# A two-layer decoder trunk in float32: part of the input is turned by VectorE instead of TensorE, and the model dimension is renumbered to suit

## The chip, the cores and the metric

The kernel runs on one core of a Trainium2 chip. The engines that matter here are TensorE (PE; its weight loads have rows of their own, PEld), VectorE (DVE), ScalarE (ACT), GpSimd (POOL) and SyncE (SP), which issues nearly all DMAs. The metric is the device time of one execution in microseconds; a comparison uses the median of several runs.

## The reference, cut to what matters

```python
def reference(x, ...):                       # x (1, 1024, 1024) float32
    h = x
    # layer 0: HGRN2 mixer (w_in: 1024 -> 4096), layer norm, gated ConvFFN, layer norm
    mix = hgrn2_mixer(h, hgrn_w_in[0], lower_bounds[0], hgrn_gnorm_w[0], hgrn_w_out[0])   # h @ w_in first
    h = layer_norm(ALPHA * h + mix, ...)
    h = layer_norm(ALPHA * h + conv_ffn(h, ...), ...)
    k, v = split(h @ shared_w_kv)            # 1024 -> 512, once
    # layer 1: sliding-window attention (w_q: 1024 -> 1024), layer norm, gated ConvFFN, layer norm
    mix = swa_sink_mixer(h, k, v, swa_w_q[0], swa_sinks[0], bias, mask, swa_w_out[0])
    ...
    return h
```

Each product `h @ w` sums over the 1024 model features d. In which order and grouping the sum visits d is free, as long as h and w agree.

## The kernel before, in words

TensorE sums over partitions, so both operands of `h @ w` must have features on the 128 partitions. The weights lie so in memory (a row is a feature). The activations come as rows of tokens and must be turned: `T` holds the turned activations, `T[p, 0, kc, t]` the rounded high part and `T[p, 1, kc, t]` the low part of token t and feature 128·kc + p, for eight groups kc = 0..7 (`KC` = 8). A float32 product is made of three passes, high·high, high·low and low·high, so everything is split in two before it is multiplied. `split` does that: ScalarE writes the rounded copy (line 221), VectorE writes the difference (`low_part`, line 169).

The tokens are eight row blocks (`tb` = 0..7) of 128. `x_load` brings one block of x, 512 KB, into `Y[:, tb, :]`, tokens on partitions. `x_block` (blocks 0 and 1) and `turn_block` (blocks 2 to 7) turn a block: eight TensorE transposes (`tr`, line 204; the block's 128 by 128 piece is the stationary operand, the identity the moving one) into PSUM, then one split from PSUM into `T`. `turn_block` is also called by `ln_mid`, which turns the eight row blocks of h between the two layers; there the products with `shared_w_kv` and `swa_w_q` follow. The FFNs and the rest turn their data by code of their own.

The beginning of the program, in order. SyncE issues x block 0, two weight units `raw0` and `raw1` (512 KB each in two DMAs, `ig_load`), x blocks 1 to 5, the forget-gate weights `f`, x blocks 6 and 7, the query weights `q` and the masks. `first_rows` (line 752) multiplies blocks 0 and 1 while the weights are still being split; between its passes the generator `ahead` (`x_first`) places the transposes of blocks 1, 2 and 3. `ig_block` then does two row blocks per step, tp = 1, 2, 3 (lines 714 and 715: for each kc a 512-wide matmul with the high part of `T` and a 256-wide one with the low part), and during steps tp = 1 and 2 `x_pair` places the transposes of the next two blocks. After them `qf` multiplies with the f and q weights.

Every engine here works through its instructions in the order in which the program writes them (`tc.manual_schedule`). `od` (class `Order`) is a clock kept while the program is written: matmuls advance it, `od.spawn` starts a generator at a delay, and `od.tick` after each matmul group resumes those that are due. So the numbers behind `yield` and in `spawn` only set where instructions are written. `lower_bounds` computes a small table (`lbt`) from a transpose of `pr` (line 824) and some VectorE and ScalarE operations of 8 to 17 columns.

Of the kernel before, what the change touches and what calls it, by code (L numbers as in the profile page):

```python
# [13 lines left out]
AF = mybir.ActivationFunctionType  # L14
ALU = mybir.AluOpType

P = 128
S = 1024
D = 1024
NB = S // P  # L20
KC = D // P
# [86 lines left out]
def trunk(ctx: ExitStack, tc: tile.TileContext, a: dict, out: bass.AP):  # L108
    nc = tc.nc
    PS = bass.MemoryType.PSUM  # L110
    od = Order()
# [10 lines left out]
    nhalf = cp.tile([P, 1], F32, name="nhalf")  # L122
# [5 lines left out]
    T = cp.tile([P, 2, KC, S], F32R, name="T")  # L128
    Y = cp.tile([P, 8, D], F32, name="Y")
# [10 lines left out]
    def psmm():  # L140
        return mmp.tile([P, 512], F32, name="psmm")

    def psax():
        return axp.tile([P, 1024], F32, name="psax")
# [12 lines left out]
    def hl_at(i):  # L157
        return HL[:, 2 * i:2 * i + 2, :]
# [8 lines left out]
    def low_part(lo, src, hi, eng):  # L167

        make = lambda e: e.tensor_tensor(lo, src, hi.bitcast(F32), op=ALU.subtract)  # L169
        if isinstance(eng, list):  # L170
            eng.append(lambda: make(nc.vector))
        else:
            return make(eng or nc.vector)
# [29 lines left out]
    def tr(ps, src):  # L203
        nc.tensor.transpose(ps, src, ident)  # L204
        od.t += 0.109
# [14 lines left out]
    def split(hi, lo, src, eng=None):  # L220
        nc.scalar.copy(hi, src)  # L221
        return low_part(lo, src, hi, eng)
# [35 lines left out]
    def turn_block(tb):  # L258

        ps = psax()  # L260
        for kc in range(KC):
            tr(ps[:, kc * P:(kc + 1) * P], Y[:, tb, kc * P:(kc + 1) * P])
        ts = slice(tb * P, (tb + 1) * P)
        split(T[:, 0, :, ts], T[:, 1, :, ts], ps.rearrange("p (k t) -> p k t", k=KC))

    def ln_mid(tb):
        yield 11.0 if tb < 4 else 22.0
        turn_block(tb)
# [379 lines left out]

    x = a["x"][0]
    w_in = a["hgrn_w_in"][0]  # L650
    w_iv = w_in.rearrange("(kc p) c -> p kc c", p=P)
    hgrn_pool = tc.tile_pool(name="hp", bufs=1, reuse_waits="tile")
    with tc.tile_pool(name="t", bufs=1, reuse_waits="tile") as raws, hgrn_pool as hp:
        raw_tail(raws)

        def ig_load(h, u):
            return load(lambda r: [(r.rearrange("p (k g c) -> p k g c", k=4, g=2)[:, :, g, :],
                                    w_iv[:, 4 * u:4 * u + 4, (2 + g) * D + h * P:(2 + g) * D + (h + 1) * P])
                                   for g in range(2)])
# [4 lines left out]
        def qf_load(h, g):  # L664
            c0 = g * D + h * P
            return load(lambda r: [(r.rearrange("p (k c) -> p k c", k=KC), w_iv[:, :, c0:c0 + P])])
# [55 lines left out]
        def soon_all(left=0):  # L722
            while len(soon) > left:
                od.finish([soon.pop(0)])

        def ig_first(raw):

            hl = hl_at(ring["hl"] % 6)
            ring["hl"] += 1
            by_gate = lambda t: t.rearrange("p (k g c) -> p k g c", k=4, g=2)  # L730
            for g in range(2):
                nc.vector.tensor_copy(by_gate(hl[:, 0])[:, :, g, :], by_gate(raw)[:, :, g, :])
            low_part(hl[:, 1], raw, hl[:, 0], nc.gpsimd)
            return hl.rearrange("p h (k c) -> p h k c", k=4)

        def ig_second(raw):

            hl = hl_at(ring["hl"] % 6)
            ring["hl"] += 1
            for k in range(2):  # L740
                nc.scalar.copy(hl[:, 0, 512 * k:512 * (k + 1)], raw[:, 512 * k:512 * (k + 1)])
            low_part(hl[:, 1], raw, hl[:, 0], None)
            return hl.rearrange("p h (k c) -> p h k c", k=4)
# [26 lines left out]
        with tc.tile_pool(name="ep", bufs=1, reuse_waits="tile") as ep:  # L770
            pr = ep.tile([17, P], F32, name="pr")

            def x_load(tb):
                nc.sync.dma_start(Y[:, tb, :], x[tb * P:(tb + 1) * P, :])

            def x_block(tb):
                ts = slice(tb * P, (tb + 1) * P)
                halves = [psmm() for _ in range(2)]
                for k in range(KC):
                    tr(halves[k // 4][:, k % 4 * P:(k % 4 + 1) * P], Y[:, tb, k * P:(k + 1) * P])  # L780
                for i, ps in enumerate(halves):
                    ks = slice(4 * i, 4 * i + 4)
                    split(T[:, 0, ks, ts], T[:, 1, ks, ts], ps.rearrange("p (k t) -> p k t", k=4))

            def x_pair(tb):
                yield 0.0
                turn_block(tb)
                yield 0.5
                turn_block(tb + 1)

            warm = sm.tile([P, 1], F32, name="warm")
            mf = hp.tile([P, 7 * BL + P], F32, name="kd")
            nc.gpsimd.dma_start(pr[:16, :], a["hgrn_lb_logits"].rearrange("r (k p) -> (r k) p", p=P))
            nc.gpsimd.dma_start(pr[16:17, :], a["hgrn_gnorm_w"])
            with tc.manual_schedule(engines={EN.PE, EN.SP, EN.Activation, EN.DVE}):
                nc.scalar.activation(warm, nhalf, AF.Exp)
                x_load(0)
                raw0 = ig_load(0, 0)
                raw1 = ig_load(0, 1)
                for tb in range(1, 4):  # L800
                    x_load(tb)
                us = [ig_first(raw0)]
                lm = ep.tile([P, NH], F32, name="lm")
                le = ep.tile([P, 2, NH], F32, name="le")

                idle = psmm()
                for n in (9, 3):
                    for _ in range(n):
                        nc.tensor.matmul(idle[:, :P], still, still, start=True, stop=True)
                    if n == 9:  # L810
                        x_block(0)
                us.append(ig_second(raw1))

                def x_first():
                    x_block(1)
                    yield 1.0
                    turn_block(2)
                    yield 1.2
                    turn_block(3)

                def lower_bounds():
                    yield 0.0
                    ps = psmm()
                    nc.tensor.transpose(ps[:, :17], pr, ident[:17, :17])
                    nc.vector.tensor_copy(par, ps[:, :17])
                    nc.vector.tensor_tensor(lm, par[:, 0:8], par[:, 8:16], op=ALU.max)
                    for r in range(2):
                        nc.vector.tensor_tensor(le[:, r, :], par[:, 8 * r:8 * r + 8], lm, op=ALU.subtract)
                    nc.scalar.activation(le, le, AF.Exp)
                    nc.scalar.activation(warm, nhalf, AF.Sigmoid)  # L830
                    nc.vector.tensor_tensor(lm, le[:, 0, :], le[:, 1, :], op=ALU.add)
                    nc.vector.reciprocal(lm, lm)
                    nc.vector.tensor_tensor(lbt[:, 0, :], le[:, 0, :], lm, op=ALU.mult)
                    nc.vector.tensor_scalar(lbt[:, 1, :], lbt[:, 0, :], -1.0, 1.0, op0=ALU.mult, op1=ALU.add)

                bounds = od.spawn(lower_bounds(), 4.9)
                ahead = x_first()
                ig_block(0, us, 0, ahead=ahead)
                od.finish([od.spawn(ahead), bounds])
                for tb in range(4, 6):  # L840
                    x_load(tb)
                raws0 = {"f": qf_load(0, 1)}
                for tb in range(6, NB):
                    x_load(tb)
                raws0["q"] = qf_load(0, 0)
                nc.sync.dma_start(mf, a["masks"])
                w0 = {}
                for tp in range(1, NB // 2 - 1):
                    ahead = od.spawn(x_pair(2 * tp + 2), 2.0)
                    ig_block(0, us, tp)  # L850
                    od.finish([ahead])
                    soon_all(1)
                w0["f"] = qf_split(raws0["f"])
                ig_block(0, us, NB // 2 - 1)
                w0["q"] = qf_split(raws0["q"])
                soon_all()
                nc.vector.tensor_copy(msk, mf)
# [347 lines left out]
        with tc.manual_schedule(engines={EN.PE, EN.SP, EN.Activation, EN.DVE, EN.Pool}):  # L1205
# [89 lines left out]
            ps = psax()  # L1295
# [26 lines left out]
    with (tc.tile_pool(name="ta", bufs=1, reuse_waits="tile") as raws,  # L1322
# [6 lines left out]
        sk, nsk = sinks[:, :16], sinks[:, 16:32]  # L1329
        nc.scalar.dma_start(sk, bass.AP(tensor=a["swa_sinks"].tensor, offset=0, ap=[[0, P], [1, 16]]))  # L1330
        wkv = a["shared_w_kv"]
        wkvv = wkv.rearrange("(kc p) c -> p kc c", p=P)
        Kl = at.tile([P, 2, S], F32R, name="Kl")
        Vt = at.tile([P, NB, 256], F32, name="Vt")
        khl, uv = [], []
# [25 lines left out]
            proj_tok(uv, tp, ps)  # L1361
            nc.scalar.copy(Vt[:, 2 * tp:2 * tp + 2, :], ps.rearrange("p (a b) -> p a b", a=2))

        wq = a["swa_w_q"][0].rearrange("(kc p) (h e) -> p kc h e", p=P, e=64)

        W0 = at.tile([P, 2, 4, P], F32, name="W0")
        bfs = {}
# [145 lines left out]
        with tc.manual_schedule(engines={EN.PE, EN.Activation, EN.DVE, EN.Pool}):  # L1513
# [7 lines left out]
            q, done = next(g)  # L1521
# [20 lines left out]
            for c in range(8):  # L1542
                fill = q_proj(hl) if c < 7 else last_filler()
                nq, nd = next(fill)
                for bp in range(0, 4, 2):
                    n = 2 * c + bp // 2
# [48 lines left out]
                q = nq  # L1595
            for _ in range(2):
                ps = psax()
# [49 lines left out]
```

## Time and profile before

| | |
|---|---|
| median of 3 runs | 2131.9 us (2131.87 to 2132.25) |
| the profiled execution | 2131.04 us, span 2129.3 us |
| PE busy | 2119.9 us (100%), 12663 matmuls |
| PEld busy | 1779.6 us (84%) |
| DVE busy | 1760.9 us (83%) |
| ACT busy | 926.5 us (44%) |
| POOL busy | 132.5 us (6%) |
| PE clock granted | 0.999 |
| DMA | 278.96 MB, mean 131 GB/s |

A row of the page's groups names line, engine, operation, output<-inputs, shape and count, then busy time and mean duration of one, then the idle time before it and what ended that. In names of matmuls the moving operand stands first behind the arrow, the stationary one second. A row of the chain that ended last has start, length and what ran; lengths there do not overlap, so they add up to the span. In the windows view each engine's busy time in a stretch is given with its number of instructions.

### The profile page before, as it was taken

Reading aid. Unit: us, or ns where it says so; the run is one execution under the profiler, and the core shown is the slowest. Engines: PE = TensorE matmul, PEld = TensorE weight load, DVE = VectorE, ACT = ScalarE, POOL = GpSimd, SP = SyncE. Lnnn points to the kernel's source line nnn. Section 1 sums busy time; section 2 is a strip of 40 time slices with the busy share of each in tenths; the row PEclk is TensorE's granted clock in tenths of the full one; section 3 lists DMA queues with packets and bytes.
Section 4 is the critical chain, followed back from the end, with each engine's and each line's share of the span. In section 5 each row is a group of like instructions: output and inputs, shape, how many; then the busy total and the mean of one; then the engine's idle time right before and its main releaser. Section 6 shows DMA issues by size and latency. Waiting matters only on the chain.

```text
span 2129.3 us, 32129 instructions
## 1 busy us (share of the span) xinstructions
PE 2119.9 (100%) x12663; PEld 1779.6 (84%) x12663; DVE 1760.9 (83%) x2375; ACT 926.5 (44%) x1491; POOL 132.5 (6%) x150
## 2 busy tenths in 40 slices
PE   9999999999999999999999999999999999999998
PEld 8888888888888888888888888888888888888887
DVE  4777776677999999887988658969999999978986
ACT  4444444452444444434433356743544444444430
POOL 1000000001100000000001113321000000000002
PEclk9999999999999999999999999999999999999999
DMA  5655443214223222228854411042233222249662
GB/s 216 243 211 169 144 132 119 75 32 177 99 85 98 85 89 79 80 99 275 288 190 161 129 26 45 24 149 89 80 100 98 90 86 83 86 148 325 229 215 90
DMA packets 229838, 278.96 MB, mean 131 GB/s; under 512 B 29960, under 2 KB 158648, under 8 KB 226872
## 3 DMA queue, kind: packets, MB, share of 16 engines
q1 hardware_dynamic: 228736, 276.53, 39.0%
q8 instruction: 99, 1.62, 0.3%
q10 hardware_dynamic: 856, 0.37, 0.1%
q14 instruction: 51, 0.42, 0.1%
q0 software_dynamic: 96, 0.02, 0.0%
HBM read 213.94 MB, written 62.94 MB: 130 GB/s over the span
## 4 chain that ended last, share of the span: by engine, by line
PE 99%; DMA 0%; DVE 0%; SPq 0%; issue 0%; DVEq 0%
PE psmm L194 17%; PE psmm L196 17%; PE psmm L195 17%; PE psax L194 10%; PE psax L196 10%; PE psax L195 10%; PE psmm L714 5%; PE psax L200 4%; PE psmm L715 3%; PE psmm L204 1%; PE psmm L200 1%; PE psax L204 1%; PE psax L1427 1%; PE psmm L1274 1%; DMA Y<-in_x_dram 0%; PE psmm L752 0%
## 5 line engine op out<-in xcount | busy, mean ns | idle before, releaser
L194 PE MATMUL psmm<-T,HL 128*128 128x512 f32 x768 | 303.4, 395 | 0.0
L196 PE MATMUL psmm<-T,HL 128*128 128x512 f32 x768 | 299.4, 390 | 0.0
L195 PE MATMUL psmm<-T,HL 128*128 128x512 f32 x768 | 299.2, 390 | 0.0
L473 DVE SCALAR_TENSOR_TENSOR Y<-Y,cwt 128x1023 f32<-128x1023 f32 (+1 forms) x176 | 225.0, 1281 | 44.3 <-ACT Y L471 42.9
L221 ACT CAST HL<-rx 128x1024 fp32r<-128x1024 f32 (+1 forms) x151 | 150.7, 1007 | 178.3 <-PE psmm L195 30.9
L169 DVE TENSOR_TENSOR HL<-rx,HL 128x1024 fp32r<-128x1024 f32 (+1 forms) x151 | 178.5, 1188 | 16.9 <-ACT HL L221 16.8
L714 PE MATMUL psmm<-HL,T 128*128 128x512 f32 x496 | 176.8, 399 | 0.0
L196 PEld LDWEIGHTS psmm<-T,HL 128*128 128x128 f32 x768 | 144.2, 188 | 30.7
L194 PEld LDWEIGHTS psmm<-T,HL 128*128 128x128 f32 x768 | 144.3, 188 | 29.6 <-issue 0.4
L195 PEld LDWEIGHTS psmm<-T,HL 128*128 128x128 f32 x768 | 144.3, 188 | 28.8 <-issue 0.4
L471 ACT ACTIVATE Y<-Y,cwt 128x1024 f32<-128x1024 f32 x88 | 108.7, 1238 | 101.6 <-DVE Y L460 89.4
L715 PE MATMUL psmm<-HL,T 128*128 128x256 f32 x496 | 138.9, 280 | 0.0
L194 PE MATMUL psax<-T,HL 128*128 128x512 f32 x352 | 137.3, 390 | 0.0
L196 PE MATMUL psax<-T,HL 128*128 128x512 f32 x352 | 137.0, 389 | 0.0
L195 PE MATMUL psax<-T,HL 128*128 128x512 f32 x352 | 137.0, 389 | 0.0
L243 POOL TENSOR_TENSOR rs<-rs,nhalf 128x1 f32<-128x1 f32 x32 | 44.6, 1394 | 1286.6 <-DVE rs L242 1286.6
L714 PEld LDWEIGHTS psmm<-HL,T 128*128 128x128 f32 x496 | 93.1, 188 | 21.0
L715 PEld LDWEIGHTS psmm<-HL,T 128*128 128x128 f32 x496 | 93.7, 189 | 0.4
L221 ACT CAST HT<-rx 128x1024 fp32r<-128x1024 f32 (+1 forms) x37 | 35.5, 960 | 127.9 <-DVE rx L427 76.4
L169 DVE TENSOR_TENSOR HL<-raw,HL 128x1024 fp32r<-128x1024 f32 x51 | 62.1, 1219 | 20.2 <-ACT HL L176 19.3
L195 PEld LDWEIGHTS psax<-T,HL 128*128 128x128 f32 x352 | 66.2, 188 | 13.7
L196 PEld LDWEIGHTS psax<-T,HL 128*128 128x128 f32 x352 | 66.1, 188 | 13.6
(315 smaller groups left out, 5232.3 us busy)
## 6 DMA issues: line engine op xcount, KB each, us to landing
rx<-in_ffn_w_in_dram SPq DMA_DIRECT2D x136, 256.0 KB, 3.2
rx<-gd SPq DMA_DIRECT2D x118, 256.0 KB, 3.9
Y<-in_ffn_w_out_dram SPq DMA_DIRECT2D x44, 512.0 KB, 6.4
bsd<-Y SPq DMA_DIRECT2D x22, 1024.0 KB, 4.8
gd<-Y SPq DMA_DIRECT2D x44, 512.0 KB, 2.6
rx<-in_ffn_w_out_dram SPq DMA_DIRECT2D x54, 256.0 KB, 4.7
R<-bsd SPq DMA_DIRECT2D x44, 256.0 KB, 5.1
Y<-in_ffn_w_in_dram SPq DMA_DIRECT2D x40, 256.0 KB, 2.9
```

The lines of the kernel that those rows point to most:

```text
L169: make = lambda e: e.tensor_tensor(lo, src, hi.bitcast(F32), op=ALU.subtract)
L194: nc.tensor.matmul(ps, st(0), mv(0), start=start, stop=False)
L195: nc.tensor.matmul(ps, st(0), mv(1), start=False, stop=False)
L196: nc.tensor.matmul(ps, st(1), mv(0), start=False, stop=stop)
L200: nc.tensor.matmul(ps, lhsT, rhs, start=start, stop=stop, **kw)
L204: nc.tensor.transpose(ps, src, ident)
L221: nc.scalar.copy(hi, src)
L243: nc.gpsimd.tensor_tensor(rs, rs, nhalf, op=ALU.pow)
L471: nc.scalar.activation(c, u, AF.Identity, bias=cwt[:, l, 3, ci:ci + 1], scale=cwt[:, l, 2, ci:ci + 1])
L473: nc.vector.scalar_tensor_tensor(c[:, sh:], u[:, :S - sh], cwt[:, l, 2 - sh, ci:ci + 1], c[:, sh:], op0=ALU.mult, op1=ALU.add)
L714: nc.tensor.matmul(ps, T[:, 0, kc, ts], w[:, :, kc % 4, :], start=kc == 0, stop=False)
L715: nc.tensor.matmul(ps[:, :256], T[:, 1, kc, ts], w[:, 0, kc % 4, :], start=False, stop=kc == KC - 1)
```

## The change

Four things change together.

1. Features are grouped as 8p + k instead of 128·k + p: `T[p, ., k, t]` now holds feature 8p + k. `turn_block` and `x_block` therefore take `Y[:, tb, kc::KC]`, every eighth column, as stationary operand, and the weights `hgrn_w_in`, `shared_w_kv` and `swa_w_q` are read by `"(p kc) c -> p kc c"`, eight neighbouring rows per partition.
2. x blocks 3 to 7 are no longer turned by TensorE. Their loads put column quarter q (256 columns) onto partitions 32q to 32q + 31, with token t of a 32-token group on partition 32q + t (`quarters`: four DMAs, one block at a time for block 3, two blocks at a time for 4, 5 and 6, 7). A VectorE transpose of 32 by 32 squares (`turn_squares`, line 274 after) then gives the turned block in one instruction, written over `Y[:, tb - 3, :]`, which is free by then. It reads every eighth column within a square, 32 bytes apart, and writes contiguously.
3. The split of these blocks (`split_turned`) reads the turned block from SBUF instead of PSUM.
4. The order at the beginning is rewritten: SyncE issues all of blocks 3 to 5 before f; the transpose of `pr` moves ahead; `lower_bounds` is cut in two around its ScalarE operation; the turn of block t + 1 stands behind the split of block t.

```diff
 def turn_block(tb):
-            tr(ps[:, kc * P:(kc + 1) * P], Y[:, tb, kc * P:(kc + 1) * P])
+            tr(ps[:, kc * P:(kc + 1) * P], Y[:, tb, kc::KC])
...
+    def quarters(to, rows):
+        for q in range(4):
+            nc.sync.dma_start(to[q * 32:(q + 1) * 32].rearrange("p (b d) -> p b d", b=rows.shape[0] // 32),
+                              rows[:, q * 256:(q + 1) * 256].rearrange("(b t) d -> t b d", t=32))
+    def turn_squares(src, turned):
+        nc.vector.transpose(turned.rearrange("p (k b t) -> p b k t", k=KC, b=4),
+                            src.rearrange("p (b d k) -> p b k d", b=4, k=KC))
+        od.vec(1.1)
+    def split_turned(tb, turned):
+        ts = slice(tb * P, (tb + 1) * P)
+        split(T[:, 0, :, ts], T[:, 1, :, ts], turned.rearrange("p (k t) -> p k t", k=KC))
+        od.vec(1.2)
...
-    w_iv = w_in.rearrange("(kc p) c -> p kc c", p=P)
+    w_iv = w_in.rearrange("(p kc) c -> p kc c", p=P)
...
+            def x_quarters(tb, n):
+                quarters(Y[:, tb:tb + n, :].rearrange("p n d -> p (n d)"), x[tb * P:(tb + n) * P, :])
+            def x_turn(tb):
+                turn_squares(Y[:, tb, :], Y[:, tb - 3, :])
+            def x_split(tb):
+                split_turned(tb, Y[:, tb - 3, :])
...
             def x_pair(tb):
-                yield 0.0
-                turn_block(tb)
-                yield 0.5
-                turn_block(tb + 1)
+                for t in (tb, tb + 1):
+                    x_split(t)
+                    if t < NB - 1:
+                        x_turn(t + 1)
+                    yield 2.0
...
                 def x_first():
                     x_block(1)
+                    x_turn(3)
+                    lower_logits()
                     yield 1.0
                     turn_block(2)
+                    nc.scalar.activation(le, le, AF.Exp)
+                    x_split(3)
+                    nc.scalar.activation(warm, nhalf, AF.Sigmoid)
                     yield 1.2
-                    turn_block(3)
+                    x_turn(4)
+                    lower_bounds()
...
-        wkvv = wkv.rearrange("(kc p) c -> p kc c", p=P)
+        wkvv = wkv.rearrange("(p kc) c -> p kc c", p=P)
...
-        wq = a["swa_w_q"][0].rearrange("(kc p) (h e) -> p kc h e", p=P, e=64)
+        wq = a["swa_w_q"][0].rearrange("(p kc) (h e) -> p kc h e", p=P, e=64)
```

How the instructions move. On TensorE, from the first transposes of x to the first `ig_block`, the rows before are these (`psmm<-ident,Y` and `psax<-ident,Y` are transposes of a row block, `psmm<-ident,pr` the one of the small table, line 752 is `first_rows`):

```order
L204 MATMUL psmm<-ident,Y 128x128 x8
L752 MATMUL psmm<-HL,T 128x256 x16
L204 MATMUL psax<-ident,Y 128x128 x8
L752 MATMUL psmm<-HL,T 128x256 x4
L824 MATMUL psmm<-ident,pr 128x17
L752 MATMUL psmm<-HL,T 128x256 x4
L204 MATMUL psax<-ident,Y 128x128 x8
L752 MATMUL psmm<-HL,T 128x256 x8
L714 MATMUL psmm<-HL,T 128x512
```

And after (line 770 is `first_rows`, line 732 the first matmul of `ig_block`):

```order
L204 MATMUL psmm<-ident,Y 128x128 x8
L846 MATMUL psmm<-ident,pr 128x17
L770 MATMUL psmm<-HL,T 128x256 x16
L204 MATMUL psax<-ident,Y 128x128 x8
L770 MATMUL psmm<-HL,T 128x256 x16
L732 MATMUL psmm<-HL,T 128x512
```

The transposes of block 3 are gone, those of the table stand right behind block 1, and block 2 stands after 16 `first_rows` matmuls as before. Further on, the four groups of eight transposes between the `ig_block` matmuls (blocks 4 to 7) are gone too. From there to the end TensorE has the same instructions in the same order.

On VectorE, from the low part of block 3 to the last of `ig_block`'s second step, before (`T<-psax` are low parts of row blocks 3 to 7, read from PSUM; `VG` are values of `ig_block`):

```order
L169 TENSOR_TENSOR T<-psax,T 128x8x128
L699 TENSOR_TENSOR VG<-VG,psmm 128x2x128
L169 TENSOR_TENSOR T<-psax,T 128x8x128 x2
L679 TENSOR_TENSOR VG<-VG,psmm 128x256 x2
L169 TENSOR_TENSOR T<-psax,T 128x8x128
L689 TENSOR_TENSOR VG<-VG,sg 128x2x128
L169 TENSOR_TENSOR T<-psax,T 128x8x128
L679 TENSOR_TENSOR VG<-VG,psmm 128x256
```

And after, the start of that stretch (`Y<-Y` is the transpose of squares, `T<-Y` the low part of a block turned by it, `par`, `lm` and `le` the small table):

```order
L274 STREAM_TRANSPOSE Y<-Y 128x4x8x32
L847 COPY par<-psmm 128x17
L848 TENSOR_TENSOR lm<-par 128x8
L850 TENSOR_TENSOR le<-par,lm 128x8 x2
L169 TENSOR_TENSOR T<-psax,T 128x8x128
L169 TENSOR_TENSOR T<-Y,T 128x8x128
L274 STREAM_TRANSPOSE Y<-Y 128x4x8x32
```

and its end, blocks 5 to 7:

```order
L169 TENSOR_TENSOR T<-Y,T 128x8x128
L274 STREAM_TRANSPOSE Y<-Y 128x4x8x32
L697 TENSOR_TENSOR VG<-VG,psmm 128x256
L169 TENSOR_TENSOR T<-Y,T 128x8x128
L274 STREAM_TRANSPOSE Y<-Y 128x4x8x32
L697 TENSOR_TENSOR VG<-VG,psmm 128x256
L169 TENSOR_TENSOR T<-Y,T 128x8x128
```

The turn of block 3 now stands ahead of the small table and of the low part of block 2; from block 4 on, low part and turn alternate.

More of the change, by code (lines that the diff above doesn't have):

```diff
@@ L779, in x_block @@
                 for k in range(KC):
-                    tr(halves[k // 4][:, k % 4 * P:(k % 4 + 1) * P], Y[:, tb, k * P:(k + 1) * P])
+                    tr(halves[k // 4][:, k % 4 * P:(k % 4 + 1) * P], Y[:, tb, k::KC])
                 for i, ps in enumerate(halves):
@@ L799, in trunk @@
                 raw1 = ig_load(0, 1)
-                for tb in range(1, 4):
+                for tb in range(1, 3):
                     x_load(tb)
+                x_quarters(3, 1)
+                x_quarters(4, 2)
                 us = [ig_first(raw0)]
@@ L812, in trunk, with lower_logits @@
                 us.append(ig_second(raw1))
[L814 to L818, printed above, removed]
-                    turn_block(3)
-                def lower_bounds():
-                    yield 0.0
+                def lower_logits():
                     ps = psmm()
@@ L828, in lower_bounds @@
                         nc.vector.tensor_tensor(le[:, r, :], par[:, 8 * r:8 * r + 8], lm, op=ALU.subtract)
-                    nc.scalar.activation(le, le, AF.Exp)
-                    nc.scalar.activation(warm, nhalf, AF.Sigmoid)
+                def lower_bounds():
                     nc.vector.tensor_tensor(lm, le[:, 0, :], le[:, 1, :], op=ALU.add)
@@ L834, in lower_bounds, with x_first @@
                     nc.vector.tensor_scalar(lbt[:, 1, :], lbt[:, 0, :], -1.0, 1.0, op0=ALU.mult, op1=ALU.add)
-                bounds = od.spawn(lower_bounds(), 4.9)
+                def x_first():
+                    x_block(1)
+                    x_turn(3)
+                    lower_logits()
+                    yield 1.0
+                    turn_block(2)
+                    nc.scalar.activation(le, le, AF.Exp)
+                    x_split(3)
+                    nc.scalar.activation(warm, nhalf, AF.Sigmoid)
+                    yield 1.2
+                    x_turn(4)
+                    lower_bounds()
                 ahead = x_first()
                 ig_block(0, us, 0, ahead=ahead)
-                od.finish([od.spawn(ahead), bounds])
-                for tb in range(4, 6):
-                    x_load(tb)
+                od.finish([od.spawn(ahead)])
                 raws0 = {"f": qf_load(0, 1)}
-                for tb in range(6, NB):
-                    x_load(tb)
+                x_quarters(6, 2)
                 raws0["q"] = qf_load(0, 0)
@@ L848, in trunk @@
                 for tp in range(1, NB // 2 - 1):
-                    ahead = od.spawn(x_pair(2 * tp + 2), 2.0)
+                    ahead = od.spawn(x_pair(2 * tp + 2), 0.5)
                     ig_block(0, us, tp)
```

## The prediction

> **What bounds the kernel now.** First the page's busy times and the chain that ended last by engine, then the waits of TensorE, two groupings over the whole run.
>
> ```profile
> span 2129.3 us, 32129 instructions
> PE 2119.9 (100%) x12663; PEld 1779.6 (84%) x12663; DVE 1760.9 (83%) x2375; ACT 926.5 (44%) x1491; POOL 132.5 (6%) x150
> PE 99%; DMA 0%; DVE 0%; SPq 0%; issue 0%; DVEq 0%
> PE psmm L809 <- DVE Y L760: 1.0, 1, 1.0
> PE psmm L204 <- DMA Y<-in_x_dram: 0.5, 1, 0.5
> ```
>
> TensorE is the chain. It waits twice, 1.0 us at the very start and 0.5 us for x block 1; after that, for some 2119 us, never. So what is taken off TensorE shortens the run one for one, and what makes TensorE wait lengthens it one for one, wherever it is. VectorE's 83% is no bound as long as its results come in time; the change loads VectorE just there, so the question is local: the first 40 us. The chain in order of time there (start, length, what):
>
> ```profile
> 10.24 1.06 PE psmm L204 x8
> 11.30 1.91 PE psmm L752 x16
> 13.22 0.87 PE psax L204 x8
> 14.09 0.47 PE psmm L752 x4
> 14.73 0.67 PE psmm L752 x4
> 15.39 0.87 PE psax L204 x8
> 16.27 0.96 PE psmm L752 x8
> ...
> 22.20 0.23 PE psmm L714
> ...
> 26.79 0.23 PE psmm L714
> ...
> 28.72 0.87 PE psax L204 x8
> ```
>
> A turned row block costs the chain 0.87 us, 0.109 for a transpose. Thirteen kc steps lie between the L714 rows at 22.20 and 26.79: 0.353 each, so a row block of `ig_block` takes 8 x 0.353 = 2.83 us. That is the pace at which TensorE will ask for blocks 2 to 7.
>
> **The change part by part.** *Removed from TensorE.* Blocks 3 to 7, five rows of which the first (15.39) and the last (28.72) stand above: 5 x 0.87 = 4.35 us, all on the path. And the last 16 matmuls of line 752, cut in three before (0.47 + 0.67 + 0.96 = 2.10), run in one piece (1.91): 0.19. Together 4.54, the most that the change can bring.
>
> *The 11 row blocks that TensorE still turns* (x blocks 0 to 2 and the eight of `ln_mid`, 88 transposes) load their stationary operand from columns 32 bytes apart. No stationary operand of the trace is spread so. What a weight load has to spare is seen when shapes are compared (mean ns of one behind the comma):
>
> ```profile
> L204 PEld LDWEIGHTS psax<-ident,Y 128*128 128x128 f32 x112 | 12.7, 140 | 0.7
> L200 PEld LDWEIGHTS psax<-VG,A 128*128 128x128 f32 x128 | 19.1, 191 | 0.5
> L200 PEld LDWEIGHTS psax<-kd 128*32 128x32 f32 x768 | 12.5, 110 | 5.5 <-issue 4.5 <-ACT A L1048 0.6 <-ACT fg L900 0.4
> ```
>
> Ordinary loads take 110 ns for 32 columns and 191 for 128, so 0.84 ns a column over about 83 fixed. A transpose's load of 128 columns takes 140, so about 57 ns of columns: half. It hides under the transpose's 109 ns. If the spread doubles the 57, it becomes an ordinary load's 107, and the row for that is line 752 above: 128-column loads beside matmuls of 256 columns run at 1.91 / 16 = 0.119 us. Bounds: nothing, or 0.010 x 88 = 0.9 us. I take 0.3, nearer to nothing, since the 57 has 50 ns of cover. If that cover is gone it is rival C.
>
> *Added to VectorE.* Five transposes of squares, each 128 x 1024. The trace has none. Nearest rows:
>
> ```profile
> L732 DVE CAST HL<-raw 128x512 fp32r<-128x512 f32 x2 | 0.9, 428 | 4.6 <-DMA raw<-in_hgrn_w_in_dram 4.6
> L169 DVE TENSOR_TENSOR T<-psax,T 128x1024 fp32r<-128x1024 f32 x14 | 17.1, 1220 | 12.1 <-ACT T L221 12.1
> L1010 DVE TENSOR_TENSOR kd<-kp,qp 128x512 f32<-128x512 f32 x16 | 10.3, 685 | 0.0
> L933 DVE COPY_PREDICATED Ab<-msk,psax 128x128 f32<-128x128 uint8 x24 | 10.7, 446 | 0.8
> L954 DVE COPY_PREDICATED Ab<-msk,psax 128x128 f32<-128x128 uint8 x24 | 7.1, 295 | 0.3
> L221 ACT CAST T<-Y 128x1024 fp32r<-128x1024 f32 x10 | 10.2, 1049 | 0.0
> ```
>
> A plain copy passes 512 columns in 0.43 us, so 1024 in 0.69 to 0.86 (an estimate: with about 0.16 fixed, or none): the low bound. The tensor_tensor of the same size takes 1.22. L1010 reads `kp` in steps of 16 bytes, each element twice, and at 685 ns for 512 columns it is no slower per column than the 1.22 for 1024; L933 and L954 write as many elements, L933 in steps of 8 or 16 bytes, and it takes 0.15 us more for 128, or 1.18 ns an element: 1024 of those would add 1.21, so 2.43 us is the high bound. I take 1.22: a pass over as many elements, and the tensor_tensor that steps 16 bytes shows no loss. [...]
>
> *The loads.* x blocks 3 to 7 come in 12 DMAs to 32 partitions each instead of 5 to 128. The nearest rows are windows with loads to 64 partitions (`swa_w_out`, 1410 to 1424) and to 128 (`hgrn_w_out` and x, 480 to 490); the last two figures are DMA share and GB/s:
>
> ```profile
> 1410.00:1424.00 14.00, 14.00 (x86) 11.49 (x85) 3.14 (x3) 3.46 (x4) 0.00 (x0) 1.00 0.75 220
> 480.00:490.00 10.00, 10.00 (x49) 8.35 (x49) 2.68 (x4) 1.55 (x4) 0.33 (x1) 1.00 1.02 398
> L164 SPq DMA_DIRECT2D rx<-in_swa_w_out_dram x16: 465/594/598, 1412.0 to 1423.8; - x16
> ```
>
> So 220 to 398 GB/s. [...] Up to block 1, which TensorE waited for until 10.2, SyncE's queue is unchanged. Block 2 (524 KB at 398: 1.3 us) is there at 11.4, block 3 at 12.7 to 13.8, blocks 4 and 5 at 15.4 to 18.6, f 1.3 later, 6 and 7 at 19.4 to 24.7. SyncE issues seven DMAs more; at the 0.59 us of the last row that is 4 us, spent while earlier loads still run; f and q, behind them, are wanted only when block 7 is multiplied, at 16.4 + 6 x 2.83 = 33.4.
>
> *The weights' new row order* fetches the same 512-byte pieces for other partitions. Weights with another row length (22 KB against 16) land in the same time, so I cost it at nothing, bounds 0.2 us either way; behind the start TensorE never waits for weights.
>
> ```profile
> raw<-in_hgrn_w_in_dram SPq DMA_DIRECT2D x32, 256.0 KB, 3.4
> rx<-in_ffn_w_in_dram SPq DMA_DIRECT2D x136, 256.0 KB, 3.2
> ```
>
> *The new waits.* Now the engines' queues are walked in their new order, with handovers of 0.04 us.
>
> ```profile
> 4.32 0.50 POOL L794 DMA_DIRECT2D pr<-in_hgrn_gnorm_w_dram  x1
> pr<-in_hgrn_gnorm_w_dram POOLq DMA_DIRECT2D x1, 0.5 KB, 5.7
> 11.52 1.29 DVE L169 TENSOR_TENSOR T<-psmm,T 128x512 fp32r<-128x512 f32 x2 [1.55 <-ACT T L221]
> 14.13 1.01 ACT L221 CAST T<-psax 128x1024 fp32r<-128x1024 f32 x1 [2.15 <-PE psax L204]
> 16.31 0.17 DVE L825 COPY par<-psmm 128x17 f32<-128x17 f32 x1
> 16.72 0.24 DVE L828 TENSOR_TENSOR le<-par,lm 128x8 f32<-128x8 f32 x2
> 17.23 1.28 ACT L830 ACT_TABLE_LOAD   x1
> 19.53 0.39 ACT L696 ACTIVATE VG<-psmm 128x256 f32<-128x256 f32 x1
> ```
>
> TensorE: block 1 ends at 11.30; the table's transpose, whose input landed at 4.32 + 5.7 = 10.0, adds 0.17 (the gap from 14.56 to 14.73 in the chain); 16 matmuls, block 2 ends at 14.25, 16 more to 16.16. ScalarE has the high part of block 2 at 15.31. VectorE is free at 12.81; it turns block 3 when that has landed (14.0 to 15.0), makes the table's first rows (16.31 to 16.96: 0.65) and then the low part of block 2, done at 16.6 to 16.9. Behind the waiting transpose stand just these; who waits for them is TensorE, which wants that low part at 16.16 + 0.23 = 16.39: **0.2 to 0.6 us lost**. Block 3's low part is done 1.2 later, in time. Block 4 is turned from 17.9 (or 18.6, when landed) and its low part is done at 21.4 to 22.2, wanted at 22.2 to 22.6: in time. Then the chain turn 1.22, high part 1.05, low part 1.22, with three handovers 3.6 us per block, is slower than TensorE's 2.83: 0.74 us lost per block once the lead is used up. Block 5 loses 0 to 0.4, block 6 0.7, block 7 0.7. Together 1.6 to 2.4 us given back; I take 2.0. Before, VectorE idled 12.1 us ahead of its 14 low parts out of PSUM (the L169 row); that slack is what the turns use up.
>
> ScalarE's table load (1.28) and two gate operations (0.39 each), now between the high parts of blocks 3 (done at 16.6) and 4, end at 18.8, before block 4 is turned.
>
> *The sum.* -4.54 + 2.0 + 0.3 = -2.24 us. The profiled execution would go from 2131.04 to 2128.8 (its span from 2129.3 to 2127.1); it lies 0.9 below the median of the runs, so the median goes from 2131.9 to 2129.7.
>
> **The rivals.** *A (the forecast):* -4.54 + (1.6 to 2.4) + (0 to 0.9): 2129.0 to 2130.7, wider when the transpose lies between its bounds.
>
> *B: VectorE becomes the bound of the beginning.* With 2.43 us for a transpose the loop is 4.8 us per block against 2.83; 1.95 is lost for each of blocks 5, 6 and 7, 0.5 for 4 and 0.7 to 1.8 for 2: 7.1 to 8.1. Result -4.54 + (7.1 to 8.1) + (0 to 0.4) = +2.6 to +4.0: 2134.5 to 2135.9. It ends above before from a transpose of about 1.8 us. For it: L933 against L954. Against it: L1010. [...]
>
> *C: TensorE reads the spread stationary operand so slowly that the load sets the pace.* If the 57 ns of columns became 218, eight transposes would cost 0.87 us more. Block 0's 0.87 falls into the wait for block 1; the ten others are 8.7: -4.54 + 1.6 + 8.7 = +5.8, 2137.7. It ends above before from 145 ns a transpose (80 x 0.036 = 2.9). Against it: it takes nearly four times the columns' time. [...]
>
> *D: full gain.* With a transpose at the copy's 0.69 us the loop takes 3.0 us, block 4's lead of 0.8 covers that to the end, and at most the 0.2 at block 2 remains: 2127.4 to 2127.6, and up to 0.9 more for the stationary operands.
>
> *E: quarter loads at half the 64-partition rate,* 110 GB/s: blocks 4 and 5 land at 26, 6 and 7 at 37; TensorE waits 3.0, 4.4 and 4.6 us for them at blocks 2, 4 and 6 and 0.7 at 5 and 7: +8.9, 2140.8. Against it: 220 GB/s in the 64-partition window came at a DMA share of 0.75, so the queues were not even full.
>
> **How the numbers follow.** A 0.58, B 0.17, C 0.13, D 0.08, E 0.04. Predicted is A's 2129.7. The range holds A, B and D, 2127.4 to 2135.9, and leaves out C and E, 0.17. A measurement of this kernel can tell about 0.2%, 4.3 us, from no change: below 2127.6 or above 2136.2. The first needs most of D, 0.06; the second is C, E and B's edge, 0.18; within lie A, nearly all of B and the rest of D, 0.76. The likeliest case alone: 2128.2 to 2131.5.
>
> **What would show it.** In the profile after: 5 groups of eight transposes fewer before 40 us; transposes of squares at 1.2 us each, or at 2.4 (B) or 0.7 (D); rows "PE <- DVE T L169" with a loss at blocks 2, 6 and 7; line 204 in the chain at 0.87 to 0.95 for eight (A) or 1.7 (C); x quarters landing by 19 and 25. Wrong it is if the transposes take 1.2 and TensorE still loses more than 3 us, or if waits appear behind 40 us.

## The result and the profile after

The changed kernel takes 2134.8 us (median of 20 runs, 2133.3 to 2137.1), the kernel before 2131.6 on the same chip (20 runs, 2130.2 to 2132.3): ratio 1.0015, 95% interval 1.0009 to 1.0022. That is 3.2 us slower (1.9 to 4.7), inside the range of the prediction but on the other side of no change from its forecast of 2.2 us faster. 2134.8 is where rival B stood (2134.5 to 2135.9); the range held it because it was drawn to take in B, to which the prediction gave a chance of 0.17.

The page's head, and TensorE's waits over the whole run (total us, times, longest), of the changed kernel:

```profile
span 2132.6 us, 32070 instructions
PE 2118.0 (99%) x12623; PEld 1775.8 (83%) x12623; DVE 1770.7 (83%) x2380; ACT 926.6 (43%) x1491; POOL 133.0 (6%) x150
```

```profile
PE psmm L733 <- DVE T L169: 3.8, 5, 1.2
PE psmm L732 <- ACT T L221: 1.6, 3, 0.9
PE psmm L839 <- DVE Y L778: 1.0, 1, 1.0
PE psmm L770 <- ACT HL L759: 0.4, 1, 0.4
```

Forty transposes fewer, 1.9 us less of busy TensorE, and eight new waits, for the high and low parts of turned blocks (L732, L733 are the matmuls of `ig_block`, L714 and L715 before). All of them lie before 40 us. There the chain in order of time (start, length, what) has changed hands:

```profile
4.94 6.65 DMA Y<-in_x_dram
11.61 7.67 DMA Y<-in_x_dram
19.41 2.21 DVE Y L274
21.65 1.06 ACT T L221
22.73 1.23 DVE T L169
23.96 2.12 DVE Y L274
...
32.85 2.10 DVE Y L274
34.95 0.31 DVE VG L697
35.62 1.04 ACT T L221
36.68 1.24 DVE T L169
37.96 0.39 PE psmm L733
...
40.78 0.23 PE psmm L194
```

The same place in the chain of the kernel before, where the multiplication by f and q begins:

```profile
37.71 0.24 PE psmm L194
```

So 3.07 us are lost up to there; the span grew by 3.3. Up to 19.3 us the chain is the loading of x. From 19.4 to 38 us it is turn, high part, low part, turn: VectorE and ScalarE set the end, and TensorE follows. VectorE's timeline shows the two turns that had to wait for their data, those of blocks 3 and 4:

```profile
13.91 2.17 DVE L274 STREAM_TRANSPOSE Y<-Y 128x1024 f32<-128x1024 f32 x1 [1.14 <-DMA Y<-in_x_dram]
19.41 2.21 DVE L274 STREAM_TRANSPOSE Y<-Y 128x1024 f32<-128x1024 f32 x1 [0.34 <-DMA Y<-in_x_dram]
```

Two groups of the changed kernel (VectorE's turn; TensorE's load of the strided stationary operand, to which e3 below returns):

```profile
L274 DVE STREAM_TRANSPOSE Y<-Y 128x1024 f32<-128x1024 f32 x5 | 10.9, 2190 | 1.5 <-DMA Y<-in_x_dram 1.5
L204 PEld LDWEIGHTS psax<-ident,Y 128*128 128x128 f32 x72 | 9.1, 193 | 0.3
```

A turn takes 2.19 us, not 1.22. What it costs TensorE is seen at the first low-part matmul of each block in TensorE's timeline (start, length; in brackets the idle time before and its releaser):

```profile
17.81 0.39 PE L733 MATMUL psmm<-HL,T 128*128 128x256 f32 x1 [1.22 <-DVE T L169]
24.01 0.39 PE L733 MATMUL psmm<-HL,T 128*128 128x256 f32 x1 [0.29 <-DVE T L169]
28.46 0.39 PE L733 MATMUL psmm<-HL,T 128*128 128x256 f32 x1 [0.76 <-DVE T L169]
32.90 0.39 PE L733 MATMUL psmm<-HL,T 128*128 128x256 f32 x1 [0.76 <-DVE T L169]
37.96 0.39 PE L733 MATMUL psmm<-HL,T 128*128 128x256 f32 x1 [0.77 <-DVE T L169]
```

These are blocks 2, 4, 5, 6 and 7. At TensorE's own 2.83 us a block, block 4 was due at 17.81 + 5.66 = 23.47 and blocks 5 to 7 each 2.83 behind the one before: late by 0.5, 1.6, 1.6 and 2.2; block 2 was due at 16.43 (`ig_block` begins at 16.20) and is 1.4 late. Sum 7.4. Another 0.2 is lost ahead of them: `ig_block` began at 17.06 before, and without the 0.87 and 0.19 that were removed there it would begin at 16.00, not 16.20. 7.6 - 4.54 is the 3.07.

The idle time that the waits above show is less, 5.4 us in all. It counts from the modelled end of the matmul before, and behind a matmul that waited the next one starts later than in the running row (18.04 behind 17.81, where elsewhere it is 0.11 us); so the lateness is read from the starts. The same reckoning, from the first matmul of `ig_block` to L194 in TensorE's timeline, less 17.01 us for that stretch before without its four turned blocks, is used for the experiments below and called what TensorE loses.

### The profile page after: what moved, and what is told of

It reads as the page before. It is cut to its first block, busy times and chain, and to the rows that moved or that the text cites. A ratio compares the mean times of both kernels' runs of the same rounds, so it can differ in the third digit from the quotient of the medians.

```text
span 2132.6 us, 32070 instructions
## 1 busy us (share of the span) xinstructions
PE 2118.0 (99%) x12623; PEld 1775.8 (83%) x12623; DVE 1770.7 (83%) x2380; ACT 926.6 (43%) x1491; POOL 133.0 (6%) x150
## 4 chain that ended last, share of the span: by engine, by line
PE 98%; DVE 1%; DMA 1%; ACT 0%; SPq 0%; issue 0%; DVEq 0%; ACTq 0%
PE psmm L194 17%; PE psmm L196 17%; PE psmm L195 17%; PE psax L194 10%; PE psax L195 10%; PE psax L196 10%; PE psmm L732 5%; PE psax L200 4%; PE psmm L733 3%; PE psmm L204 1%; PE psmm L200 1%; PE psax L1458 1%; PE psax L204 1%; PE psmm L1305 1%; DMA Y<-in_x_dram 1%; DVE Y L274 0%
## 5 line engine op out<-in xcount | busy, mean ns | idle before, releaser
L194 PE MATMUL psmm<-T,HL 128*128 128x512 f32 x768 | 303.3, 395 | 0.0
L732 PE MATMUL psmm<-HL,T 128*128 128x512 f32 x496 | 176.9, 399 | 1.6 <-ACT T L221 1.6
L196 PEld LDWEIGHTS psmm<-T,HL 128*128 128x128 f32 x768 | 144.2, 188 | 30.6
L194 PEld LDWEIGHTS psmm<-T,HL 128*128 128x128 f32 x768 | 144.2, 188 | 29.8 <-issue 0.4
L733 PE MATMUL psmm<-HL,T 128*128 128x256 f32 x496 | 139.4, 281 | 3.8 <-DVE T L169 3.8
L194 PE MATMUL psax<-T,HL 128*128 128x512 f32 x352 | 137.3, 390 | 0.0
L732 PEld LDWEIGHTS psmm<-HL,T 128*128 128x128 f32 x496 | 93.1, 188 | 23.4 <-ACT T L221 2.6
L733 PEld LDWEIGHTS psmm<-HL,T 128*128 128x128 f32 x496 | 93.7, 189 | 5.6 <-DVE T L169 5.4
L196 PEld LDWEIGHTS psax<-T,HL 128*128 128x128 f32 x352 | 66.1, 188 | 13.7
L194 PEld LDWEIGHTS psax<-T,HL 128*128 128x128 f32 x352 | 66.1, 188 | 13.7
L195 PEld LDWEIGHTS psax<-T,HL 128*128 128x128 f32 x352 | 66.0, 188 | 13.5
```

Source lines behind the costliest of these rows:

```text
L194: nc.tensor.matmul(ps, st(0), mv(0), start=start, stop=False)
L195: nc.tensor.matmul(ps, st(0), mv(1), start=False, stop=False)
L196: nc.tensor.matmul(ps, st(1), mv(0), start=False, stop=stop)
L732: nc.tensor.matmul(ps, T[:, 0, kc, ts], w[:, :, kc % 4, :], start=kc == 0, stop=False)
L733: nc.tensor.matmul(ps[:, :256], T[:, 1, kc, ts], w[:, 0, kc % 4, :], start=False, stop=kc == KC - 1)
```

## The experiments

Six kernels ran, in two groups, each beside the kernel before on the same chip: its median was 2130.97 us in the first group (27 runs) and 2131.3 in the second (21).

**e1: one turn for each step.** Each of the five turns reads its squares in another way; the result is not x turned. Only the durations are read. Theory S says that the step of the read sets the time, rival W that a transpose of 4-byte elements is simply as slow as in the changed kernel (2.19 us), whatever the step.

```diff
+        if tb == 3:    # step 8 elements, as in the changed kernel
+            o, i = ... "p (k b t) -> p b k t" ..., ... "p (b d k) -> p b k d" ...
+        elif tb == 4:  # step 1, the same strided order of the squares written
+            o, i = ... "p (k b t) -> p b k t" ..., ... "p (b k d) -> p b k d" ...
+        elif tb == 5:  # step 2
+            o, i = ... "p (m s t) -> p m s t" (s=2), ... "p (m d s) -> p m s d" (s=2)
+        elif tb == 6:  # step 4
+            o, i = ... "p (m s t) -> p m s t" (s=4), ... "p (m d s) -> p m s d" (s=4)
+        else:          # step 1, squares written in order
+            o, i = ... "p (m t) -> p m t", ... "p (m d) -> p m d"
...
```

> The changed kernel, but each VectorE transpose of squares reads with another step: block 3 as in the changed kernel (8 elements, 32 bytes), block 4 step 1, block 5 step 2, block 6 step 4 with the writes contiguous, block 7 step 1 with reads and writes both contiguous. Blocks 4 to 7 are so permuted wrongly, only durations are read. [...] Theory W (a transpose of 4-byte elements costs 2.1 ns per element whatever the step): all five at 2.1 to 2.2.

VectorE's timeline of e1 (start, length), in the order of the branches above:

```profile
13.32 2.20 DVE L284 STREAM_TRANSPOSE Y<-Y 128x1024 f32<-128x1024 f32 x1 [0.38 <-DMA Y<-in_x_dram]
18.42 1.24 DVE L284 STREAM_TRANSPOSE Y<-Y 128x1024 f32<-128x1024 f32 x1
21.92 1.24 DVE L284 STREAM_TRANSPOSE Y<-Y 128x1024 f32<-128x1024 f32 x1
26.32 2.07 DVE L284 STREAM_TRANSPOSE Y<-Y 128x1024 f32<-128x1024 f32 x1 [0.82 <-DMA Y<-in_x_dram]
30.64 1.24 DVE L284 STREAM_TRANSPOSE Y<-Y 128x1024 f32<-128x1024 f32 x1
```

Steps 1 and 2 take 1.24 us, step 4 takes 2.07, step 8 takes 2.20: theory S holds, W falls. Reading elements 16 bytes apart already costs nearly all (2.07 of 2.20); how the squares are written costs nothing at step 1 (1.24 in both orders). One run, 2131.67 us.

**e2: the changed kernel with turns at step 1.** Loads, orders and strided stationary operands stay; the features come out permuted.

```diff
-                            src.rearrange("p (b d k) -> p b k d", b=4, k=KC))
+                            src.rearrange("p (b k d) -> p b k d", b=4, k=KC))
```

> The changed kernel, but all five transposes of squares read contiguously (step 1), same writes; the features come out permuted, only the time is read. Same instructions in the same order. Theory S: transposes 1.2 us, TensorE loses 3 to 4 us at blocks 2 and 4 to 7 instead of 7.3, time 0.6 to 1.2 us below before. Theory W: transposes 2.19, time as the changed kernel, 3 us above before.

2130.53 us (2129.28 to 2133.81, 11 runs), ratio 0.9999 (0.9991 to 1.0008): -0.4 against before. The group of the turns, and where L194 starts in the chain:

```profile
L274 DVE STREAM_TRANSPOSE Y<-Y 128x1024 f32<-128x1024 f32 x5 | 6.2, 1243 | 1.8 <-DMA Y<-in_x_dram 1.8
```

```profile
36.06 0.23 PE psmm L194
```

The step alone takes L194 from 40.78 back to 36.06. Of these 4.7 us, 0.5 is an earlier beginning of this execution (`ig_block` starts at 15.74 against 16.20); the rest is what TensorE loses, 3.1 instead of 7.4. So the step is the cause of the slowdown. The 3 to 4 us expected come out; a gain in the time does not, since behind L194 this execution loses 1.0 us again: 0.2 at `ln_mid`, 0.3 in a wait of L204 for VectorE, and the rest is open.

The turns now wait for their data, 1.8 us in all, and the wait at block 6 reaches TensorE (VectorE's timeline, then TensorE's):

```profile
25.46 1.25 DVE L274 STREAM_TRANSPOSE Y<-Y 128x1024 f32<-128x1024 f32 x1 [0.58 <-DMA Y<-in_x_dram]
29.09 0.38 PE L733 MATMUL psmm<-HL,T 128*128 128x256 f32 x1 [0.75 <-DVE T L169]
```

Block 2 loses 0.4, block 6 1.4 and block 7 1.3, blocks 4 and 5 nothing.

**e3: the weights' order alone.** The kernel before with features 8p + k in transposes and weights, nothing else.

```diff
-            tr(ps[:, kc * P:(kc + 1) * P], Y[:, tb, kc * P:(kc + 1) * P])
+            tr(ps[:, kc * P:(kc + 1) * P], Y[:, tb, kc::KC])
...
-    w_iv = w_in.rearrange("(kc p) c -> p kc c", p=P)
+    w_iv = w_in.rearrange("(p kc) c -> p kc c", p=P)
...
```

> The kernel before with the feature order 8p + k alone: TensorE turns all 16 row blocks from columns 32 bytes apart, weights are read in the new row order, x comes in whole rows, nothing on VectorE. If the new weight order costs nothing: 16 row blocks x 0.025 us = 0.4 us, plus up to 0.4 at the cold block 0: 0.2 to 0.8 us above before. If the weight order or the spread operand is what made the changed kernel slower: 3 us above before.

2131.28 us (2130.85 to 2132.48, 11 runs), ratio 1.0002 (0.9993 to 1.0011). Its load of the strided operand:

```profile
L204 PEld LDWEIGHTS psax<-ident,Y 128*128 128x128 f32 x112 | 14.0, 193 | 0.5
```

The load grows from 140 to 193 ns and stays nearly hidden: eight transposes take 0.89 to 0.90 us in the chain of e3, too. In the chain of the changed kernel, at `ln_mid` (the first and the last of its eight groups):

```profile
1162.59 0.89 PE psax L204 x8
...
1218.57 0.90 PE psax L204 x8
```

0.87 became 0.89 to 0.90, so eight blocks lose 0.2 us. The 0.2 to 0.8 us expected fit the +0.3 of the medians, which is not told from no change. The renumbering does not explain the result.

**e4: step 1, and whole rows.** e2, with x blocks 3 to 7 loaded one by one to 128 partitions; what is turned is then not x in any order.

```diff
             def x_quarters(tb, n):
-                quarters(Y[:, tb:tb + n, :].rearrange("p n d -> p (n d)"), x[tb * P:(tb + n) * P, :])
+                for t in range(tb, tb + n):
+                    x_load(t)
```

> As e2_step1, and blocks 3 to 7 are loaded in whole rows (5 DMAs to 128 partitions) instead of column quarters; the data is then not turned rightly, only the time is read. Theory S: loads run at 350 to 400 GB/s again, the loss at blocks 2 and 4 goes, 1.6 us are lost in all: 2.5 us below before. Theory W: block 4 is turned 2 us earlier, about 2.5 us less lost than in the changed kernel: 0.5 to 1 us above before.

2128.82 us (2128.42 to 2130.46, 11 runs), ratio 0.9991 (0.9982 to 1.0000): -2.15 against before, at the edge of what can be told from no change, with L194 here in the chain:

```profile
35.48 0.23 PE psmm L194
```

That is 2.23 before the 37.71. With turns of 1.24 us, near the 1.22 that the forecast took, and with the loads of before, the forecast's -2.24 comes out, but in part by luck: TensorE loses the forecast's 2.0, as 0.4 at block 2, 0.3 at block 6 and 1.3 at block 7, where the forecast had 0.2 to 0.6 at block 2, 0 to 0.4 at block 5 and 0.7 each at 6 and 7, and it had counted with loads by quarters. Block 6 in TensorE's timeline of e4:

```profile
28.55 0.39 PE L733 MATMUL psmm<-HL,T 128*128 128x256 f32 x1 [0.26 <-DVE T L169]
```

The loads in the windows view of the changed kernel, then of e4 (the last two figures are DMA share and GB/s):

```profile
10.00:15.00 5.00, 5.00 (x44) 4.85 (x42) 3.03 (x4) 1.59 (x3) 0.00 (x0) 1.00 1.11 226
15.00:20.00 5.00, 3.78 (x25) 3.22 (x24) 4.51 (x8) 3.67 (x7) 0.00 (x0) 1.00 1.17 222
20.00:25.00 5.00, 4.71 (x27) 3.85 (x26) 4.47 (x7) 1.05 (x1) 0.00 (x0) 1.00 1.15 208
```

```profile
10.00:15.00 5.00, 5.00 (x44) 4.85 (x43) 3.63 (x8) 1.48 (x3) 0.00 (x0) 1.00 1.04 397
15.00:20.00 5.00, 4.78 (x32) 4.13 (x31) 4.10 (x7) 4.50 (x8) 0.00 (x0) 1.00 1.08 382
```

In windows where mostly quarters are loaded, 208 to 226 GB/s are moved at a DMA share of 1.11 to 1.17, with whole rows 382 to 397. What that costs at step 1: TensorE loses 3.1 us in e2 and 2.0 in e4, and the 1.1 between them stand at block 6, whose turn waited for x in e2 alone. L194 is only 0.6 apart (36.06 against 35.48) because e2's execution began `ig_block` 0.6 earlier. The medians are 1.7 apart; what lies behind L194, where the two kernels are alike, is open.

At step 8 no run has whole rows. In the changed kernel the turns of blocks 3 and 4 waited 1.14 and 0.34 us at the head of the chain, so quicker loads might have saved up to 1.5 us there, an estimate; 7.6 - 1.5 - 4.54 is still 1.6 above before.

**f3: the turn ahead of the low part.** The changed kernel with two orders exchanged: the turn of the next block stands ahead of the split, so that ScalarE's high part runs beside it, and the quarters of blocks 6 and 7 are asked for ahead of f.

```diff
                 for t in (tb, tb + 1):
-                    x_split(t)
                     if t < NB - 1:
                         x_turn(t + 1)
+                    x_split(t)
                     yield 2.0
...
-                raws0 = {"f": qf_load(0, 1)}
                 x_quarters(6, 2)
+                raws0 = {"f": qf_load(0, 1)}
```

> The changed kernel with two orders exchanged and nothing else: VectorE turns block t+1 before it makes the low part of block t, so that ScalarE's high part of a block runs beside the next turn; and the quarters of blocks 6 and 7 are asked for ahead of the f weights. Theory (the turn at steps of 8 elements, 2.19 us, sets a loop of turn, cast, low part of 4.45 us): the loop becomes VectorE's own 2.19 + 1.22 = 3.4 us against TensorE's 2.83, so blocks 5 to 7 lose about 0.6 each instead of 1.6, 1.6 and 2.2; blocks 2 and 4 lose 1.4 and 0.4 as they did. Sum -4.54 + 3.6 + 0.25 = -0.7 against the kernel before, some 3.5 us less than the changed kernel. Rival (the loads by quarters are what is late): the turns of blocks 6 and 7 wait for their data and the time stays within 1 us of the changed kernel's, +2 to +3.

2132.58 us (2130.74 to 2134.02, 11 runs), ratio 1.0006 (0.9998 to 1.0015): +1.3 against before, not told from no change, better than the changed kernel's +3.2 and 2.0 short of the -0.7 expected. TensorE's timeline of f3:

```profile
18.14 0.39 PE L733 MATMUL psmm<-HL,T 128*128 128x256 f32 x1 [2.10 <-DVE T L169]
25.50 0.39 PE L733 MATMUL psmm<-HL,T 128*128 128x256 f32 x1 [1.45 <-DVE T L169]
29.09 0.39 PE L733 MATMUL psmm<-HL,T 128*128 128x256 f32 x1 [0.53 <-DVE T L169]
32.66 0.38 PE L733 MATMUL psmm<-HL,T 128*128 128x256 f32 x1 [0.53 <-DVE T L169]
```

Blocks 5 and 6 lose 0.8 and 0.7 instead of 1.6 each, near the 0.6 expected, and block 7 only 0.2. But block 4 came at 25.50, due at 23.80: the turn of block 5 now stands ahead of its low part, which the expectation had not walked; and block 2 lost 2.2 instead of 1.4, since block 3 landed later (its turn, which waited 2.06 us for it, starts at 14.28 against 13.91) and TensorE was there earlier (15.66 against 16.20). No turn behind block 3's waits for its data, so the rival falls as it was stated; what the late block 3 costs is the loads' share here.

VectorE's own work explains why an order alone cannot save it. From block 3's landing (13.9) to where block 7's low part is wanted at TensorE's pace (16.43 + 5 x 2.83 = 30.6) are 16.7 us. Five turns of 2.19, six low parts of 1.22 and some 2 us of smaller things are 20.3, an estimate that leaves TensorE at least 3.6 late in any order, as long as block 3 lands no sooner. With turns of 1.24 it is 15.5, which fits.

**f5: two turns only.** Blocks 5 and 7 are turned by VectorE, ahead of the low parts of 4 and 6; blocks 3, 4 and 6 by TensorE from whole rows.

```diff
             def x_pair(tb):
-                for t in (tb, tb + 1):
-                    x_split(t)
-                    if t < NB - 1:
-                        x_turn(t + 1)
-                    yield 2.0
+                x_turn(tb + 1)
+                turn_block(tb)
+                yield 2.0
+                x_split(tb + 1)
+                yield 2.0
...
-                x_quarters(3, 1)
-                x_quarters(4, 2)
+                x_quarters(5, 1)
...
```

> The changed kernel with only blocks 5 and 7 turned in squares by VectorE (the turn issued ahead of the low part of block 4 or 6); blocks 3, 4 and 6 are loaded in whole rows and turned by TensorE as before. Theory (a turn of 2.19 us costs nothing where VectorE has that much free time before its result is wanted): between the low parts that TensorE wants, 2.83 us apart and 1.22 long, VectorE has 1.6 us free for each block, 3.2 for two, more than 2.19; so no low part is late, TensorE loses nothing behind block 1, and the gain is 2 x 0.87 = 1.74 less 0.25 for the strided stationary operands: -1.5 against the kernel before, ratio about 0.9993. Rival (something else in the squares costs TensorE time, such as quarter loads or the buffers that the squares go to): rows of TensorE waiting for VectorE or for x stand behind block 2 and the gain is under 0.5.

2130.65 us (2129.79 to 2131.35, 11 runs), ratio 0.9997 (0.9988 to 1.0006): -0.65 against before where -1.5 was expected, not told from no change, while the changed kernel's interval lies wholly above 1. VectorE's group, TensorE's waits and L194 in the chain:

```profile
L274 DVE STREAM_TRANSPOSE Y<-Y 128x1024 f32<-128x1024 f32 x2 | 4.4, 2203 | 0.0
```

```profile
PE psmm L838 <- DVE Y L778: 1.0, 1, 1.0
PE psmm L196 <- issue: 0.7, 1, 0.7
PE psmm L770 <- ACT HL L759: 0.4, 1, 0.4
```

```profile
35.93 0.24 PE psmm L194
```

Turns of 2.20 us cost TensorE nothing here: no row waits for VectorE in the loop, and L194 starts 1.78 earlier, about the 2 x 0.87 removed. Behind it this execution loses 0.2 at `ln_mid` and 0.7 in a gap between 100 and 200 us that the profile puts down to nothing; its span is 0.7 shorter. So the mechanism is shown at its place; a gain in the time is not.

## Why the prediction was wrong, point by point

*What bounds the kernel* held: TensorE waits nowhere behind 40 us, and what it lost before 40 went into the span one for one (+3.07, and the 0.2 of `ln_mid`).

*The 4.54 removed* held: the changed kernel's 3.07 is 7.6 lost less 4.54, and f5, which loses nothing, has L194 earlier by the two blocks that it takes off TensorE.

*The step that failed is the duration of a turn.* I took 1.22 between bounds of 0.69 and 2.43; it measured 2.19, and at 1.24 (e2) the slowdown is gone. 1.24 is what a turn costs at steps 1 and 2 (e1). The choice leaned on L1010, which steps 16 bytes at no loss (685 ns for 512 columns), but reads each element twice, so it does not show a read that steps and takes each element once; I had written down that it reads twice and still followed it. The rows that I set aside, L933 against L954, gave a bound that was off by only 0.24, but in part by luck: there the steps of 8 or 16 bytes are in what is written and in the mask, and a turn that reads in steps of 8 bytes loses nothing (1.24 us in e1, as at step 1). No row of the trace had the read in question.

*The slack* was taken too large. Of the 12.1 us that VectorE idled ahead of 14 low parts, 8.4 stand ahead of the six before 40 us (VectorE's timeline of the kernel before), the others at `ln_mid`. Five turns of 1.22 go into 8.4 us, five of 2.19 do not.

*What TensorE gives back* was 7.6 instead of 2.0, B's 7.1 to 8.1. The walk of the queues was right in kind: TensorE waits for turn, high part and low part in a row. In the sizes it was not: e2, with turns at nearly the price that I took and the loads by quarters, gives back 3.1, since the turn of block 6 waits for x and block 7 loses 1.3 instead of 0.7. B had block 4 at 0.5 and blocks 5 to 7 at 1.95; they measured 0.5, 1.6, 1.6 and 2.2. Block 7 lost the most because ScalarE's gate operation (L705, 0.42 us at 35.29) stood before its high part, which no case had; it cost some 0.6 in e2 and e4 too.

*The strided stationary operands*: taken at 0.3, measured 0.2 at the eight blocks of `ln_mid`. The load went from 140 to 193 ns; less the 83 that I had estimated as fixed, the columns' 57 became 110, the doubling that I had considered, and it stayed nearly under cover (0.87 us for eight transposes became 0.89 to 0.90). Rival C is out.

*The loads* came at the low bound: 220 was the bound, 208 to 226 measured. Block 3 was turned from 13.9 (14.0 to 15.0 said), block 4 from 19.4 (17.9, or 18.6 when landed), and in e2 block 6 only from 25.5 (landed by 24.7 said). VectorE waited 1.5 us for them in the changed kernel, at the head of the chain; so they are a second, smaller term that I had too low, 1.1 at step 1 (e2 against e4) and up to 1.5 by estimate at step 8. Rival E is out.

*The weights' order* cost nothing that e3 can show.

*Full gain, D,* would have needed turns of 0.69; even contiguous ones take 1.24 (e1).

## What to carry to other kernels

Before moving work to an engine with free time, price it at the access pattern that it will have; where no row of the trace has that pattern and the nearest rows disagree, measure it, as e1 did in one run. Compare the engine's whole work with the time until its last result is wanted: five turns of 2.19 us did not fit between 13.9 and 30.6 us by the estimate above, two did without a wait. A layout chosen to suit this transpose should leave steps of 8 bytes or less: 1.24 us at 4 and 8 bytes against 2.07 at 16 and 2.20 at 32 (e1). That alone took the loss away here but brought no gain that can be told from no change (e2); a kernel that gives right results at such a step, a grouping of features with step 2 for instance, was not tried.

## What the hardware showed that I had not expected

- VectorE's float32 transpose of 128 x 1024 in squares takes 1.24 us reading in steps of 4 or 8 bytes, 2.07 at 16 and 2.20 at 32 (e1): the loss is a jump between 8 and 16 bytes, not a slope.
- TensorE's load of a stationary operand from columns 32 bytes apart takes 193 ns instead of 140, and eight transposes 0.89 to 0.90 instead of 0.87 us (e3 and the changed kernel against the kernel before).
- The kernels that load five blocks by quarters scatter more: 3.8 us from lowest to highest in the changed kernel, 4.5 in e2, 3.3 in f3, against 2.1 before, 2.0 in e4, which differs from e2 in the loads alone, and 1.6 in f5, which loads two blocks so. Why is open.
